# Seven half-token products in place of eight for nine of the 22 gate-and-up tiles of a feed-forward block

## The chip, the cores and the metric

The kernel runs on one NeuronCore of a Trainium2 chip. The metric is the device time of one execution in microseconds (us); lower is better. TensorE (PE) multiplies; its weight loads (PEld) are shown apart from its matmuls. VectorE (DVE), ScalarE (ACT) and GpSimd (POOL) do the elementwise work, and SyncE (SP) issues most transfers.

## The reference

The reference is two blocks, each of two layers, on 512 tokens of width 1024 in float32. The first block has a recurrent layer and a top-k attention layer. The second has a windowed attention and a sparse attention, each followed by a feed-forward layer. Only the two feed-forward layers are touched here:

```python
def rms_norm(x, g):
    x32 = x.astype(jnp.float32)
    y = x32 * lax.rsqrt(jnp.mean(x32 * x32, axis=-1, keepdims=True) + RMS_EPS)
    return (y * g.astype(jnp.float32)).astype(x.dtype)

def swiglu(h, w_gu, w_down):
    gate, up = jnp.split(h @ w_gu, 2, axis=-1)
    return (jax.nn.silu(gate) * up) @ w_down

# per layer of the second block:  h = h + mixer(...);  h = h + swiglu(rms_norm(h, ffn_norm), w_gu, w_down)
```

The hidden width is 2816, which is 22 tiles of 128. So each layer has 22 gate tiles, 22 up tiles, and a down product of 22 k-tiles onto eight output tiles.

## The kernel before

All activations lie transposed: a tile is 128 features (partitions) by 512 tokens. `X[k]`, k = 0 to 7, is the residual. `Norm` holds `n.xh[k]` and `n.xl[k]`: the residual times the norm's gain, split into a rounded high part and a low remainder, each a 128x512 tile in the fast matmul type. `n.RB` is the reciprocal root-mean-square of each token, spread over the partitions; it is multiplied in after the product.

A weight tile of 1024 rows by 128 columns comes from HBM as one 128x1024 `raw` tile (512 KB, one transfer on SP's queue). It is cut into two pieces of four k-tiles (512 columns). Of each piece ACT writes the rounded high part `wh` (L133) and DVE or GpSimd the remainder `wl = raw - wh` (L134; `wpool["l"]` lists the engines, in the feed-forward layers DVE alone). The pairs (`wh`, `wl`) rotate through numbered slots: four common ones that live for the whole kernel and a number for each layer (`hl` in `open_layer`, here 4, so 8 slots); `raw` has 2 + 2 buffers.

`dense` multiplies one weight tile by eight k-tiles. For every k-tile `mm3` (L152 to L154) issues three matmuls into one PSUM bank: high by high, high by low, low by high. So a tile costs 24 matmuls with 512 moving columns.

`ffn` (L1402) is called twice. `hidden(j)`, j = 0 to 21, makes a gate product `pg` and an up product `pu` (48 matmuls). Then DVE makes g = pg*RB (L1411), ACT tanh(g/2) (L1413), DVE th = (th+1)*g (L1414), u = pu*RB (L1416) and u = th/2*u (L1417), and `split` makes the pair `hh` (ACT, L113) and `hl` (DVE, L114). `down(k0, k1, last)` multiplies a range of hidden tiles by the down weights (`dn`) and adds to `X[m]`. The order is hidden 0 to 9, down over hidden 0 to 7, hidden 10 to 17, down over 8 to 15, hidden 18 to 21, down over 16 to 21. The second layer's last down is `down_out`, in which four output tiles are made in halves of 256 tokens and the final norm follows.

Six PSUM banks (`mm`) serve the products, two (`at`) the small ones. `tmp` gives 128x512 tiles out of eight; `hh` and `hl` have 13 buffers each. The order of instructions on each engine is made by a planner that simulates the engines and picks, among what it takes to be ready, the earliest in program order; slots come free by release. So the planner, not the chip, fixes each engine's queue.

Of the kernel before, what the change touches and what calls it, by code (L numbers as in the profile page):

```python
# [10 lines left out]
F32 = mybir.dt.float32  # L11
F32R = mybir.dt.float32r
BF16 = mybir.dt.bfloat16
AF = mybir.ActivationFunctionType
ALU = mybir.AluOpType
AX = mybir.AxisListType.X
P = 128
T = 512
NB = 4
KD = 8  # L20
# [6 lines left out]
def f32(ap):  # L27
    return ap.bitcast(F32)
# [3 lines left out]
def kernel(ctx: ExitStack, tc: tile.TileContext, a: dict, out: bass.AP, upto: int = 9, start: int = 1):  # L32
    nc = tc.nc
    pe, act, dve, pool = nc.tensor, nc.scalar, nc.vector, nc.gpsimd
# [5 lines left out]
    wpool = {"ext": None, "raw": 0, "hl": 0, "nr": 0, "np": 0}  # L40
    fetched = []
    copies = []
    st = ctx.enter_context(tc.tile_pool(name="st", bufs=2))
# [9 lines left out]
    X = [XA[:, k] for k in range(KD)]  # L53
# [4 lines left out]
    def V(name, i=0, n=1, rows=slice(None)):  # L58
        o = VEC[name][0] + i
        return vec[rows, o:o + n]  # L60
# [39 lines left out]
    def ps_mm(name):  # L100

        return bank(min(psum["mm"], key=used.index), name)
# [9 lines left out]
    def split(h, l, src, eng=None):  # L112
        act.copy(h, src)  # L113
        (eng or dve).tensor_sub(l, src, f32(h))  # L114

    PC = 512

    def wtile(kind, n, dt, tags):

        base, extra = {"raw": (2, wpool["raw"]), "hl": (4, wpool["hl"])}[kind]  # L120
        c = wpool["n" + kind] = wpool.get("n" + kind, -1) + 1
        common = c % (base + extra) < base
        return [(wg if common else wpool["ext"]).tile([P, n], dt, tag=t, name=t, bufs=base if common else extra)
                for t in tags]
# [31 lines left out]
    def dense(src, xh, xl, name="mm", M=P, w=None, mid=None, among=()):  # L156

        kt = len(xh)
        h, l = w or wload(src, kt * P)
        ps = ps_mm(name)  # L160

        def part(k0, k1):
            for k in range(k0, k1):
                mm3(ps[:M], h(k * P, M), l(k * P, M), xh[k], xl[k], k == 0, k == kt - 1)

        if among:
            with tc.manual_schedule(engines={pe.engine}):
                for k in range(kt):
                    part(k, k + 1)
                    for fn in among[k * len(among) // kt:(k + 1) * len(among) // kt]:  # L170
                        fn()
            return ps
        part(0, kt // 2)
        with tc.issue_after(mid().ins) if mid else ExitStack():
            part(kt // 2, kt)
        return ps
# [62 lines left out]
    def open_layer(name, raw, hl, tmps, roles, tw=T, weng=None):  # L239
        wpool["l"] = weng or [dve]  # L240
        es = ExitStack()
        set_banks(**roles)
        if raw or hl:
            wpool["ext"] = es.enter_context(tc.tile_pool(name=name + "w", bufs=1))
        wpool["raw"], wpool["hl"], wpool["nraw"], wpool["nhl"] = raw, hl, -1, -1
        lp = es.enter_context(tc.tile_pool(name=name, bufs=1))
        tp = es.enter_context(tc.tile_pool(name=name + "t", bufs=tmps))

        def tmp(nm, w=T):
            return tp.tile([P, tw], F32, tag="t", name=nm)[:, :w]  # L250

        return es, lp, tmp
# [1147 lines left out]


    def ffn(n, layer, gname, goff, after):  # L1402
        es, lp, tmp = open_layer(f"f{layer}", 2, 4, 8, dict(mm=6, at=2))
        H = []
        nx = Norm()

        def hidden(j):
            pg = dense(a[f"w_gu{layer}"][2 * j], n.xh, n.xl, "pg")
            pu = dense(a[f"w_gu{layer}"][2 * j + 1], n.xh, n.xl, "pu")
            g = tmp("g")  # L1410
            dve.tensor_mul(g, pg, n.RB)  # L1411
            th = tmp("th")
            act.activation(th, g, AF.Tanh, scale=0.5)  # L1413
            dve.scalar_tensor_tensor(th, th, 1.0, g, op0=ALU.add, op1=ALU.mult)  # L1414
            u = tmp("u")
            dve.tensor_mul(u, pu, n.RB)  # L1416
            dve.scalar_tensor_tensor(u, th, 0.5, u, op0=ALU.mult, op1=ALU.mult)  # L1417
            h = lp.tile([P, T], F32R, tag="hh", name="hh", bufs=13)
            l = lp.tile([P, T], F32R, tag="hl", name="hl", bufs=13)
            split(h, l, u)  # L1420
            H.append((h, l))

        def down(k0, k1, last):
            def step(m, w):
                hs = H[k0:k1]
                ps = dense(None, [x[0] for x in hs], [x[1] for x in hs], "dn", w=w)
                add_res(m, ps)
                if last:
                    norm_add(nx, m, gname, goff)

            steps = [(lambda m=m: wload(a[f"w_dn{layer}"][m][:, k0 * P:k1 * P], (k1 - k0) * P),
                      lambda w, m=m: step(m, w)) for m in range(KD)]
            if last:
                run_steps(steps, after)
            else:
                for _ in range(KD):
                    run_step(steps)

        def down_out(k0, k1):


            w = {}
            rb = st.tile([P, T], F32, tag="RB", name="RB", bufs=1)

            def load(m):
                w[m] = wload(a[f"w_dn{layer}"][m][:, k0 * P:k1 * P], (k1 - k0) * P)

            def product(m, c, wd):
                hs = H[k0:k1]
                ps = ps_mm("dn")[:, :wd]  # L1450
                for i, (xh, xl) in enumerate(hs):
                    mm3(ps, w[m][0](i * P, P), w[m][1](i * P, P), xh[:, c:c + wd], xl[:, c:c + wd], i == 0,
                        i == len(hs) - 1)
                x = X[m][:, c:c + wd]
                dve.tensor_add(x, ps, x)
                sq = st.tile([P, T], F32, tag="acc" if m == 0 else "sq", name="sq", bufs=2)
                act.activation(sq[:, c:c + wd], x, AF.Square)
                if m == 0 or m == KD - 1:
                    nx.sq.append(sq)
                else:  # L1460
                    pool.tensor_add(nx.sq[0][:, c:c + wd], nx.sq[0][:, c:c + wd], sq[:, c:c + wd])
                act.activation(x, x, AF.Identity, scale=V(gname, m))

            def rms(c, wd):
                pb, _ = bcast_cols(lambda b: nx.stat[:, b:b + 1].to_broadcast([P, P]), "nrb", wd // P, ps_mm)
                act.copy(rb[:, c:c + wd], pb[:, :wd])
                return pb

            def out_half(c, wd, pb, on_pool):
                for k in range(KD):  # L1470
                    x = X[k][:, c:c + wd]
                    if k in on_pool:
                        pool.tensor_mul(x, x, rb[:, c:c + wd])
                    else:
                        dve.tensor_mul(x, x, pb[:, :wd])
                    if k % 2:
                        q = nc.sync if k % 4 == 1 else nc.scalar
                        q.dma_start(out[:, k - 1:k + 1, c:c + wd], XA[:, k - 1:k + 1, c:c + wd])

            load(0)  # L1480
            for m in range(KD):
                if m < KD - 1:
                    load(m + 1)
                if m < 4:
                    product(m, 0, T)
            with tc.manual_schedule(engines={pe.engine}):
                for m in range(4, KD):
                    product(m, 0, T // 2)
                for m in range(4, KD):
                    if m == 5:  # L1490
                        norm_stat(nx, 0, NB // 2)
                    if m == 6:
                        half = rms(0, T // 2)
                    if m == KD - 1:
                        nx.sq.pop()
                    product(m, T // 2, T // 2)
                norm_stat(nx, NB // 2, NB // 2)
                out_half(0, T // 2, half, (1,5))
                out_half(T // 2, T // 2, rms(T // 2, T // 2), (1,5))

        for j in range(10):
            hidden(j)
        down(0, 8, False)
        for j in range(10, 18):
            hidden(j)
        down(8, 16, False)
        for j in range(18, 22):
            hidden(j)
        if after:
            down(16, 22, True)  # L1510
        else:
            down_out(16, 22)
        es.close()
        return nx
# [359 lines left out]
    if start <= 1:  # L1874
        n = even()
    else:
        es, lp, tmp = open_layer("b", 0, 0, 4, dict(mm=1, at=2))
# [4 lines left out]
        n = Norm()  # L1882
# [17 lines left out]
    if start <= 5:  # L1900
        n = nsa(n)
# [150 lines left out]
```

## Time and profile before

| | |
|---|---|
| time, median of 3 runs (lowest, highest) | 1929.52 us (1928.89, 1931.39) |
| time of the profiled execution | 1933.06 us |
| its span from first to last instruction | 1931.3 us |
| mean granted TensorE clock | 0.994 of full speed |
| busy: PE, DVE, ACT, POOL | 98%, 65%, 50%, 29% of the span |
| chain that ended last: PE, DVE | 83%, 10% of the span |

The profile shows one execution. The time holds 1.8 us beside the span. A busy share is the time in which an engine has an instruction in flight; matmuls overlap in a pipeline, so what one costs is read from the starts of neighbours, not from its length.

### The profile page before, as it was taken

How to read it: one execution, taken by the hardware profiler on the slowest of the kernel's cores; microseconds unless marked ns; L12 is line 12 of the kernel's file. 1: busy time of each engine (PE TensorE's matmuls, PEld its weight loads, DVE VectorE, ACT ScalarE, POOL GpSimd, SP SyncE). 2: the span in 40 equal slices, each digit the busy share in tenths (PEclk: the TensorE clock that was granted, in tenths of full speed). 3: DMA queues.
4: the chain of work that ended last, by engine and by line, in shares of the span. 5: the costliest groups of instructions: out<-in, count | busy, mean ns of one | idle time of the engine just before them, and what ended most of it. 6: DMA issues, size and time to landing. Idle time of an engine off the chain costs nothing.

```text
span 1931.3 us, 27214 instructions
## 1 busy us (share of the span) xinstructions
PE 1889.9 (98%) x9686; PEld 1588.1 (82%) x9686; DVE 1260.8 (65%) x2586; ACT 959.4 (50%) x1975; POOL 566.9 (29%) x622
## 2 busy tenths in 40 slices
PE   9999999999998999999999999998999999999998
PEld 7888888887788887878888888888888888888887
DVE  6776667556797778796554453557999665445443
ACT  6543344424447786785332332347888543223223
POOL 1101001124457575886000000056666420000002
PEclk9999999999999999999999999999999999999999
DMA  4233342222345553211333233243111142233221
GB/s 164 87 104 119 121 123 88 89 87 78 90 131 141 146 173 116 90 44 58 139 99 98 89 97 98 66 134 116 55 60 33 44 142 90 96 98 98 94 76 60
DMA packets 72687, 189.91 MB, mean 98 GB/s; under 512 B 9252, under 2 KB 24100, under 8 KB 72552
## 3 DMA queue, kind: packets, MB, share of 16 engines
q1 hardware_dynamic: 68824, 184.43, 30.3%
q10 hardware_dynamic: 3728, 3.75, 0.6%
q8 instruction: 76, 1.25, 0.3%
q14 instruction: 59, 0.48, 0.1%
HBM read 167.03 MB, written 12.59 MB: 93 GB/s over the span
## 4 chain that ended last, share of the span: by engine, by line
PE 83%; DVE 10%; ACT 2%; DMA 2%; issue 1%; POOL 1%; SPq 1%; DVEq 0%; ACTq 0%; POOLq 0%
PE pj L152 6%; PE pj L153 6%; PE pj L154 6%; PE pg L153 4%; PE pg L152 4%; PE pg L154 4%; PE pu L152 4%; PE pu L154 4%; PE pu L153 4%; PE dn L153 4%; PE dn L152 4%; PE dn L154 4%; PE wo L152 4%; PE wo L153 3%; PE wo L154 3%; PE po L779 2%
## 5 line engine op out<-in xcount | busy, mean ns | idle before, releaser
L133 ACT CAST wh<-raw 128x512 fp32r<-128x512 f32 (+1 forms) x582 | 353.1, 611 | 616.4 <-PE dn L153 140.5
L134 DVE TENSOR_TENSOR wl<-raw,wh 128x512 fp32r<-128x512 f32 (+2 forms) x436 | 301.3, 695 | 198.6 <-ACT wh L133 191.6
L152 PE MATMUL pj<-xh,wh 128*128 128x512 f32 (+1 forms) x648 | 265.3, 410 | 0.5 <-ACT wh L133 0.5
L154 PE MATMUL pj<-xh,wl 128*128 128x512 f32 (+1 forms) x648 | 255.2, 394 | 1.4 <-DVE wl L134 0.9
L153 PE MATMUL pj<-xl,wh 128*128 128x512 f32 (+1 forms) x648 | 255.2, 394 | 1.0 <-DVE xl L281 1.0
L134 POOL TENSOR_TENSOR wl<-raw,wh 128x512 fp32r<-128x512 f32 x146 | 197.6, 1357 | 129.8 <-ACT wh L133 109.3
L289 POOL TENSOR_TENSOR sq<-sq 128x512 f32<-128x512 f32 x27 | 43.2, 1602 | 369.9 <-ACT sq L287 369.6
L154 PEld LDWEIGHTS pj<-xh,wl 128*128 128x128 f32 (+1 forms) x648 | 121.5, 188 | 29.7 <-DVE wl L134 1.3
L153 PEld LDWEIGHTS pj<-xl,wh 128*128 128x128 f32 (+1 forms) x648 | 122.2, 189 | 24.0 <-DVE xl L281 2.4
L153 PE MATMUL dn<-hl,wh 128*128 128x512 f32 (+1 forms) x376 | 141.6, 377 | 0.0
L152 PE MATMUL dn<-hh,wh 128*128 128x512 f32 (+1 forms) x376 | 141.2, 377 | 0.0
L154 PE MATMUL dn<-hh,wl 128*128 128x512 f32 (+1 forms) x376 | 140.7, 375 | 0.0
L152 PEld LDWEIGHTS pj<-xh,wh 128*128 128x128 f32 (+1 forms) x648 | 122.1, 188 | 22.3 <-ACT wh L133 1.6
L152 PE MATMUL pg<-xh,wh 128*128 128x512 f32 x352 | 138.2, 393 | 0.0
L153 PE MATMUL pg<-xl,wh 128*128 128x512 f32 x352 | 138.2, 393 | 0.0
L154 PE MATMUL pg<-xh,wl 128*128 128x512 f32 x352 | 138.2, 393 | 0.0
L152 PE MATMUL pu<-xh,wh 128*128 128x512 f32 x352 | 138.0, 392 | 0.0
L154 PE MATMUL pu<-xh,wl 128*128 128x512 f32 x352 | 138.0, 392 | 0.0
L153 PE MATMUL pu<-xl,wh 128*128 128x512 f32 x352 | 137.9, 392 | 0.0
L152 PE MATMUL wo<-yh,wh 128*128 128x512 f32 x320 | 130.7, 409 | 2.3 <-DVE vv L114 1.4
L153 PE MATMUL wo<-yl,wh 128*128 128x512 f32 x320 | 125.9, 395 | 0.0
L154 PE MATMUL wo<-yh,wl 128*128 128x512 f32 x320 | 125.7, 395 | 0.0
(413 smaller groups left out, 4401.1 us busy)
## 6 DMA issues: line engine op xcount, KB each, us to landing
raw<-in_w_gu SPq DMA_DIRECT2D x88, 512.0 KB, 3.5
raw<-in_w_even SPq DMA_DIRECT2D x48, 512.0 KB, 3.6
raw<-in_w_dn SPq DMA_DIRECT2D x32, 512.0 KB, 3.6
rsc<-rv SPq DMA_DIRECT2D x64, 160.0 KB, 3.7
raw<-in_w_eout SPq DMA_DIRECT2D x16, 512.0 KB, 3.6
stp<-rsc SPq DMA_DIRECT2D x32, 256.0 KB, 3.2
raw<-in_w_odd SPq DMA_DIRECT2D x13, 512.0 KB, 3.7
raw<-in_w_dn SPq DMA_DIRECT2D x16, 384.0 KB, 3.1
```

The costliest lines, as they stand in the source:

```text
L133: act.copy(h[:, :m], raw[:, o:o + m])
L134: eng[i % len(eng)].tensor_sub(l[:, :m], raw[:, o:o + m], f32(h[:, :m]))
L152: pe.matmul(ps, wh, xh, start=first, stop=False)
L153: pe.matmul(ps, wh, xl, start=False, stop=False)
L154: pe.matmul(ps, wl, xh, start=False, stop=last)
L289: (eng or (dve if k == KD - 1 else pool)).tensor_add(n.sq[0], n.sq[0], sq)
L779: pe.matmul(dst[:, :, 256 - w:], vv(b), p[:, :, 256 * b:256 * b + w], start=start and x + b == 0, stop=stop and x == 1 and b == nb - 1)
```

## The change

Nine of the 22 hidden tiles, j = 5, 7, 9, ..., 21, take another way to gate and up. The product is seen as a 2x2 by 2x2 block product: the two rows of blocks are gate and up, the inner index is the even or odd k-tile of a pair, and the two columns are the first and second 256 tokens. Seven block products (Strassen's scheme in its form with few additions) replace eight. Each block product is four k-tile pairs of three matmuls with 256 moving columns, so a tile has 84 such matmuls for 48 with 512.

- `scheme_weights` loads the same two raw tiles, forms four sums of weight blocks (s1 and a new a21 on GpSimd, s2 and a new a12 on DVE) and splits seven 512-column parts: seven casts on ACT, four remainders on DVE and three on GpSimd.
- `token_sums(q)`, called once for each k-tile pair in hidden 0 to 3, forms the four token-side sums: two scalings on ACT, four 128x256 subtractions on GpSimd, two splits of 512 columns.
- After the seven products ACT copies one half and DVE does seven 128x256 additions or subtractions that each read PSUM, into g and u. GpSimd multiplies g by RB and DVE u by RB; the rest of `hidden` stays.
- From j = 6 on the weight remainders of the other tiles and of the down products alternate between DVE and GpSimd.
- Eight slots for weight pairs become ten, 8 `tmp` tiles become 6, 13 `hh`/`hl` buffers become 11. The token sums take 4 x 2 tiles of 128x1024. In the other 13 tiles u = pu*RB now stands ahead of the tanh in program order.

```diff
     def ffn(n, layer, gname, goff, after):
-        es, lp, tmp = open_layer(f"f{layer}", 2, 4, 8, dict(mm=6, at=2))
+        es, lp, tmp = open_layer(f"f{layer}", 2, 6, 6, dict(mm=6, at=2))
...
+        def token_sums(q):
+            xe, xo, ta, tb = (tmp(nm) for nm in ("xe", "xo", "ta", "tb"))
+            for x, k in ((xe, 2 * q), (xo, 2 * q + 1)):
+                act.activation(x, X[k], AF.Identity, scale=V("ffn_norm", KD * layer + k))
+            t1, t2, t3, t4 = ta[:, :HT], ta[:, HT:], tb[:, :HT], tb[:, HT:]
+            pool.tensor_sub(t1, xe[:, HT:], xe[:, :HT])
+            pool.tensor_sub(t3, xo[:, HT:], xe[:, HT:])
+            pool.tensor_sub(t2, xo[:, HT:], t1)
+            pool.tensor_sub(t4, t2, xo[:, :HT])
+            h = lp.tile([P, 2 * T], F32R, name=f"th{q}")
+            l = lp.tile([P, 2 * T], F32R, name=f"tl{q}")
+            split(h[:, :T], l[:, :T], ta)
+            split(h[:, T:], l[:, T:], tb)
...
+        def scheme_weights(j):
...
+            def part(src, eng):
+                h, l = wtile("hl", PC, F32R, ("wh", "wl"))
+                hv, lv = (t.rearrange("p (q c) -> p q c", c=P) for t in (h, l))
+                act.copy(hv, src)
+                eng.tensor_sub(lv, src, f32(hv))
+                w.append((h, l))
+
+            pool.tensor_add(s1, a21, a22)
+            part(a11, dve)
+            part(a12, pool)
+            dve.tensor_sub(s2, s1, a11)
+            part(s1, dve)
+            pool.tensor_sub(a21, a11, a21)
+            part(s2, dve)
+            part(a21, pool)
+            dve.tensor_sub(a12, a12, s2)
+            part(a22, pool)
+            part(a12, dve)
...
+            for pair in plan:
+                ps = ps_mm("pw")
+                for y, rhs in enumerate(pair):
+                    h, l = w.pop(0)
+                    d = ps[:, y * HT:y * HT + HT]
+                    for q in range(KD // 2):
+                        c = slice(q * P, q * P + P)
+                        xh, xl = rhs(q)
+                        pe.matmul(d, h[:, c], xh, start=y == q == 0, stop=False)
+                        pe.matmul(d, h[:, c], xl, start=False, stop=False)
+                        pe.matmul(d, l[:, c], xh, start=False, stop=y == len(pair) - 1 and q == KD // 2 - 1)
+                    P7.append(d)
+            p1, p2, p5, p6, p7, p4, p3 = P7
...
+            act.copy(u0, p1)
+            dve.tensor_add(g0, p2, u0)
+            dve.tensor_add(u1, p6, u0)
+            dve.tensor_add(g1, p5, u1)
+            dve.tensor_add(u0, p7, u1)
+            dve.tensor_add(u1, p7, g1)
+            dve.tensor_sub(u0, u0, p4)
+            dve.tensor_add(g1, p3, g1)
 
         def hidden(j):
...
+            if j >= 5 and j % 2:
+                g, u = scheme(j)
+                pool.tensor_mul(g, g, n.RB)
+                dve.tensor_mul(u, u, n.RB)
+            else:
+                if j == 6:
+                    wpool["l"] = [dve, pool]
...
+            if j < 4:
+                token_sums(j)
...
-            h = lp.tile([P, T], F32R, tag="hh", name="hh", bufs=13)
-            l = lp.tile([P, T], F32R, tag="hl", name="hl", bufs=13)
+            h = lp.tile([P, T], F32R, tag="hh", name="hh", bufs=11)
+            l = lp.tile([P, T], F32R, tag="hl", name="hl", bufs=11)
```

## Rows read from the trace of the kernel before

**Rows 1.** Page, busy time: engine, us, share of span, instructions
```profile
PE 1889.9 (98%) x9686; PEld 1588.1 (82%) x9686; DVE 1260.8 (65%) x2586; ACT 959.4 (50%) x1975; POOL 566.9 (29%) x622
```

**Rows 2.** Page, chain that ended last, by engine
```profile
PE 83%; DVE 10%; ACT 2%; DMA 2%; issue 1%; POOL 1%; SPq 1%; DVEq 0%; ACTq 0%; POOLq 0%
```

**Rows 3.** Windows: an attention stretch, hidden 10 to 17, a down product
```profile
core 0: us, PE busy (x) PEld busy (x) DVE busy (x) ACT busy (x) POOL busy (x), PEclk, DMA share, GB/s
...
640.00:680.00 40.00, 39.30 (x280) 35.31 (x280) 27.78 (x75) 28.96 (x69) 22.18 (x20) 1.00 0.47 125
...
1069.00:1157.00 88.00, 88.00 (x383) 71.72 (x383) 46.11 (x70) 29.10 (x47) 0.00 (x0) 1.00 0.30 96
...
1157.00:1201.00 44.00, 44.00 (x194) 36.23 (x193) 17.11 (x26) 10.57 (x18) 0.00 (x0) 1.00 0.31 96
```

**Rows 4.** Timeline of PE: first matmuls of hidden 10, 11 and 12
```profile
1068.82 0.39 PE L152 MATMUL pg<-xh,wh 128*128 128x512 f32 x1
...
1080.02 0.40 PE L152 MATMUL pg<-xh,wh 128*128 128x512 f32 x1
...
1090.93 0.40 PE L152 MATMUL pg<-xh,wh 128*128 128x512 f32 x1
```

**Rows 5.** Timeline of PE: 90 half-width matmuls, 1902.65 to 1913.20
```profile
1902.65 0.28 PE L152 MATMUL dn<-hh,wh 128*128 128x256 f32 x1
...
1903.00 0.28 PE L152 MATMUL dn<-hh,wh 128*128 128x256 f32 x1
...
1903.24 0.28 PE L154 MATMUL dn<-hh,wl 128*128 128x256 f32 x1
...
1907.30 0.28 PE L152 MATMUL dn<-hh,wh 128*128 128x256 f32 x1
...
1907.64 0.28 PE L152 MATMUL dn<-hh,wh 128*128 128x256 f32 x1
...
1913.20 0.95 PE L310 MATMUL nst<-cst,sq 128*128 128x2 f32 x8
```

**Rows 6.** Timeline of weight loads in the same stretch
```profile
1903.12 0.19 PEld L154 LDWEIGHTS dn<-hh,wl 128*128 128x128 f32 x1
```

**Rows 7.** Groups of DVE, hidden 10 to 17: count, busy us, mean ns, idle before
```profile
L134 DVE TENSOR_TENSOR wl<-raw,wh 128x512 fp32r<-128x512 f32 x32 | 22.0, 687 | 11.1 <-ACT wh L133 11.1
...
L1416 DVE TENSOR_TENSOR u<-pu,RB 128x512 f32<-128x512 f32 x7 | 4.8, 691 | 11.2 <-PE pu L154 11.2
```

**Rows 8.** Groups of ACT, hidden 10 to 17
```profile
L133 ACT CAST wh<-raw 128x512 fp32r<-128x512 f32 x32 | 19.9, 622 | 46.6 <-PE pu L153 24.8 <-PE pg L153 19.3 <-PE dn L153 2.1
```

**Rows 9.** Groups of DVE and POOL by shape, 1880 to 1931
```profile
L1455 DVE TENSOR_TENSOR x<-dn,x 128x256 f32<-128x256 f32 x8 | 3.4, 424 | 11.4 <-PE dn L154 11.4
...
L1461 POOL TENSOR_TENSOR sq<-sq 128x256 f32<-128x256 f32 x6 | 4.4, 739 | 7.5 <-ACT sq L1457 7.5
L1461 POOL TENSOR_TENSOR sq<-sq 128x512 f32<-128x512 f32 x3 | 3.9, 1307 | 334.4 <-ACT sq L1457 334.4
```

**Rows 10.** Timeline of DVE around 465, while POOL works
```profile
458.87 1.79 DVE L134 TENSOR_TENSOR wl<-raw,wh 128x512 fp32r<-128x512 f32 x1
460.58 1.78 DVE L281 SCALAR_TENSOR_TENSOR xl<-x,vec,xh 128x512 fp32r<-128x512 f32 x1
...
468.65 0.68 DVE L323 TENSOR_TENSOR x<-wo,x 128x512 f32<-128x512 f32 x1
```

**Rows 11.** Timeline of POOL in the same stretch
```profile
465.18 1.74 POOL L289 TENSOR_TENSOR sq<-sq 128x512 f32<-128x512 f32 x1
466.89 1.29 POOL L134 TENSOR_TENSOR wl<-raw,wh 128x512 fp32r<-128x512 f32 x1
```

**Rows 12.** Timeline of DVE and PE after the last up product
```profile
1886.39 0.69 DVE L1416 TENSOR_TENSOR u<-pu,RB 128x512 f32<-128x512 f32 x1 [1.55 <-PE pu L154]
...
1888.70 0.69 DVE L114 TENSOR_TENSOR hl<-u,hh 128x512 fp32r<-128x512 f32 x1 [0.69 <-ACT hh L113]
...
1889.63 0.39 PE L152 MATMUL dn<-hh,wh 128*128 128x512 f32 x1
```

More of the change, by code (lines that the diff above doesn't have):

```diff
@@ L1402, in ffn @@
     def ffn(n, layer, gname, goff, after):
-        es, lp, tmp = open_layer(f"f{layer}", 2, 4, 8, dict(mm=6, at=2))
+        es, lp, tmp = open_layer(f"f{layer}", 2, 6, 6, dict(mm=6, at=2))
         H = []
         nx = Norm()
-        def hidden(j):
[L1408 to L1411, printed above, removed]
+        HT = T // 2
+        sums = []
@@ new lines, in token_sums @@
+        def token_sums(q):
[11 more added lines that the diff above has]
+            split(h[:, T:], l[:, T:], tb)
+            sums.append((h, l))
@@ new lines, in scheme_weights @@
+        def scheme_weights(j):
+            raws = []
+            for m in (2 * j, 2 * j + 1):
+                raw, = wtile("raw", 1024, F32, ("raw",))
+                nc.sync.dma_start(raw, a[f"w_gu{layer}"][m])
+                raws.append(raw.rearrange("p (q e c) -> p e q c", e=2, c=P))
+            (a11, a12), (a21, a22) = ((r[:, 0], r[:, 1]) for r in raws)
+            s1 = st.tile([P, T], F32, tag="acc", name="s1", bufs=2).rearrange("p (q c) -> p q c", c=P)
+            s2 = st.tile([P, T], F32, tag="sq", name="s2", bufs=2).rearrange("p (q c) -> p q c", c=P)
+            w = []
+            def part(src, eng):
[15 more added lines that the diff above has]
+            part(a12, dve)
+            return w
@@ new lines, in scheme, with xs, ts @@
+        def scheme(j):
+            w = scheme_weights(j)
+            def xs(k, c):
+                return n.xh[k][:, c:c + HT], n.xl[k][:, c:c + HT]
+            def ts(q, i):
+                return tuple(t[:, i * HT:i * HT + HT] for t in sums[q])
+            plan = ((lambda q: xs(2 * q, 0), lambda q: xs(2 * q + 1, 0)), (lambda q: ts(q, 0), lambda q: ts(q, 1)),
+                    (lambda q: ts(q, 2), lambda q: ts(q, 3)), (lambda q: xs(2 * q + 1, HT),))
+            P7 = []
+            for pair in plan:
[11 more added lines that the diff above has]
+            p1, p2, p5, p6, p7, p4, p3 = P7
+            g, u = tmp("g"), tmp("u")
+            g0, g1, u0, u1 = g[:, :HT], g[:, HT:], u[:, :HT], u[:, HT:]
+            act.copy(u0, p1)
[6 more added lines that the diff above has]
+            dve.tensor_add(g1, p3, g1)
+            return g, u
@@ new lines, in hidden @@
+        def hidden(j):
+            if j >= 5 and j % 2:
[5 more added lines that the diff above has]
+                    wpool["l"] = [dve, pool]
+                pg = dense(a[f"w_gu{layer}"][2 * j], n.xh, n.xl, "pg")
+                pu = dense(a[f"w_gu{layer}"][2 * j + 1], n.xh, n.xl, "pu")
+                g, u = tmp("g"), tmp("u")
+                dve.tensor_mul(g, pg, n.RB)
+                dve.tensor_mul(u, pu, n.RB)
+            if j < 4:
+                token_sums(j)
@@ L1414, in hidden @@
             dve.scalar_tensor_tensor(th, th, 1.0, g, op0=ALU.add, op1=ALU.mult)
-            u = tmp("u")
-            dve.tensor_mul(u, pu, n.RB)
             dve.scalar_tensor_tensor(u, th, 0.5, u, op0=ALU.mult, op1=ALU.mult)
-            h = lp.tile([P, T], F32R, tag="hh", name="hh", bufs=13)
-            l = lp.tile([P, T], F32R, tag="hl", name="hl", bufs=13)
+            h = lp.tile([P, T], F32R, tag="hh", name="hh", bufs=11)
+            l = lp.tile([P, T], F32R, tag="hl", name="hl", bufs=11)
             split(h, l, u)
```

## The prediction

> **What bounds the kernel now.** I read the page's busy shares and its chain first, then the windows of the feed-forward stages, then the timeline of PE in them. PE is busy for 98% of the span and is 83% of the chain that ended last [rows 1, 2]. The reader is to see in the windows that the feed-forward stages are the extreme case: PE is busy for 88.0 of 88 us at a granted clock of 1.00 (the 2.4 GHz level), while DVE has work for 46.1 us, ACT for 29.1 and POOL for none [rows 3]. ACT's weight casts there wait mostly for a PE matmul that frees a slot, 46.6 us for 32 of them [rows 8]: the weights are made ahead, and PE waits for nobody. So in these stages time is the number of matmuls times their distance, and the other engines' spare time is what the change can spend.
>
> **What the change removes on PE.** The distance comes from the starts. Hidden 10 takes 1080.02 - 1068.82 = 11.20 us, hidden 11 takes 1090.93 - 1080.02 = 10.91 [rows 4]; over 48 matmuls that is 233.3 and 227.3 ns. The alternation runs through all the later tiles, 233 ns in even ones and 227 in odd ones, so each of the nine tiles that change costs 10.91 now.
>
> For 256 moving columns the second layer's last down product has the same kind of matmul, same types and full weights: 90 of them between 1902.65 and 1913.20, 10.55 / 90 = 117.2 ns. Within it two levels are seen, (1903.24 - 1903.00) / 2 = 120 and (1907.64 - 1907.30) / 3 = 113.3 [rows 5]. A changed tile then costs 84 x 117.2 ns = 9.85 us (9.52 to 10.08). It saves 10.91 - 9.85 = 1.06 us (0.83 to 1.39), not the eighth of 1.36 us that the count of multiplications promises, because the half-width matmul costs more than half a full one. Eighteen such tiles in two layers: **-19.1 us** (-14.9 to -25.0). The saving is gone at 10.91 / 84 = 129.9 ns.
>
> A weight load lasts 0.19 us [rows 6], longer than the 0.12 us between half-width matmuls, so loads overlap each other as well as the matmuls. The rows show that they keep up. The Trainium skill's page "TensorE: Matmul & The Clock Gate", section "Back-to-back issue gap", gives a sustained spacing of pairs of load and matmul of about 81 ns at 128 columns and 131 ns at 512; by a straight line between them (an estimate) 256 columns cost 98 ns, and the changed tile would take 84 x 98 = 8.2 us where the old one took 48 x 131 = 6.3. By that rule fixed costs weigh so much that halving the columns loses; the trace has 233 and 117 ns for the same two widths, so the rule isn't borne out here.
>
> **The 26 tiles that stay.** Their two distances go with something that alternates from tile to tile, and the weight slots do so: eight slots, four for each tile. With ten slots and seven taken by a changed tile the places shift. No row tells which places give the shorter distance. If all come to 227 ns, some 22 tiles gain 0.29 us each, -6.4; if all come to 233, four tiles lose as much, +1.2. I take **-1.0**, a mixture with a few more at 227.
>
> **What the change adds, against PE's time.** A pair of one changed and one normal tile gives PE 9.85 + 11.20 = 21.05 us. In it:
> - ACT has 7 + 4 casts, 2 tanh, 2 `hh` casts at about 0.62 [rows 8] and a half-width copy, below 10 us. Half of its time stays free.
> - DVE has in the changed tile four remainders, two weight sums, u*RB, two steps of silu and `hl`: ten operations with both inputs in SBUF; in the normal tile two remainders, two steps and `hl`: five. At 0.69 [rows 7] that is 10.4 us. The seven half-width operations that read PSUM take 0.42 each [rows 9], 3.0, and g and u of the normal tile 1.4. Sum 14.7 us.
> - POOL has two sums, three remainders and g*RB, then two remainders: eight of about 1.31 [rows 9], 10.5 us.
>
> By these numbers alone every engine fits: DVE 70%, POOL 50% of PE's time. But DVE and POOL disturb each other. Where POOL works beside DVE, a DVE remainder takes 1.79 us and a scaled one 1.78, while an addition with one input in PSUM keeps 0.68 [rows 10]; POOL's own operations there take 1.74, and 1.29 when left alone [rows 11]. An operation of DVE with two SBUF inputs and one of POOL thus follow each other. The Trainium skill's page "SBUF — State Buffer", section "Who interferes with whom", states this as a lock: such a DVE instruction contends with a GpSimd instruction that reads SBUF, and the second one waits for the whole of the first. The trace agrees, with 1.79 for 0.69.
>
> The price: if each of the eight POOL operations held up one DVE operation by 1.79 - 0.69 = 1.1 us, DVE would need 14.7 + 8.8 = 23.5 us, 2.4 more than PE's 21.05; if half do, 19.1, and PE still sets the pace. Bounds over 18 pairs: 0 to +43 us. Two things pull it to the low end. DVE is free of two-input work for a third of the pair, and ten slots let weights run some six parts ahead, so only a lasting overload reaches PE. The nearest stretch with both engines loaded has DVE at 27.8 and POOL at 22.2 of 40 us, nearly these shares, and PE still at 39.3 [rows 3]. I take **+2**. Each down product, in which DVE is busy 17.1 of 44 us [rows 3], lets both engines catch up.
>
> **Token sums.** Four calls in a layer, each four ACT passes (2.5 us or a little over), four POOL operations of 0.74 [rows 9] (3.0) and two DVE remainders (1.4), in hidden 0 to 3, where PE takes over 10.9 us a tile. The spare ACT and DVE time covers them, and hidden 5 is the first user. Where the layer begins, the norm uses the same engines; if that cover is gone, the first call delays RB or the first weights by some 1 us. I take **+1** for both layers (0 to +3).
>
> **The end of hidden 21.** It changes, and the down product needs it. Now the end of the up product (PE turns to `dn` before 1886.39) is followed by u*RB at 1886.39 and `hl` at 1888.70 to 1889.39, while PE uses tiles 16 to 20 and comes to a sixth at 1889.63 [rows 12]: it arrives with 0.2 us to spare. The new chain behind the last product is an addition (0.42), g*RB on POOL (1.31), tanh, two steps, cast and remainder (0.63 + 0.69 + 0.69 + 0.62 + 0.69), 5.1 us and some 0.6 between engines, against 3.0 now. Up to 2.4 us would be late next, PE's sixth k-tile, if the queue keeps its order. The planner has five other output tiles to put in front, each 15 matmuls of 0.23 us that need only tiles 16 to 20, so the cover can be long. Between 0 and +4.8 for two layers; I take **+1**.
>
> Nothing else is on the path: the bytes and the number of transfers stay, SP's queue gets no new work, but a raw tile of a changed j is held until its last part is made. With four raw buffers the next two transfers start then, one tile (about 10 us) before they are needed. The buffers cut from 8 to 6 and 13 to 11 hold at most ten live hidden tiles and one more; only ACT or POOL would wait.
>
> **Sum.** -19.1 - 1.0 + 2 + 1 + 1 = -16.1 us. On the profiled execution's own 1933.06 that is 1917.0. It stood 3.5 above the median of the runs, so against the median: 1929.5 - 16.1 = **1913 us**, 0.8% faster. This case by itself spans 1904 to 1921: -25.0 with nothing lost, to half of the saving given back.
>
> **Rivals.**
> 1. *DVE and POOL become the bound (slower).* Place: the pairs from j = 5 on. Price: up to 2.4 us a pair, more if ACT casts also wait behind POOL's sums s1 and a21. It decides from 1.0 us for each changed tile, where 18 us are eaten. At the bound: 1929.5 - 19.1 + 1.0 + 43 = 1954. For it: DVE two-input work (10.4) and POOL work (10.5) add up to 20.9 of 21.05 us if they strictly take turns. Against: in alternation a pair of them took about 1.75, not 0.69 + 1.31, and PE held 39.3 of 40 under a like load. Full bound 0.10. A middle form, in which some 0.4 to 1.0 us a tile is lost, gives 1921 to 1931: 0.14.
> 2. *The half-width matmul costs more here than in the down product*, because weight loads surface when two token operands and seven parts alternate. If nothing overlapped, 84 x 0.19 = 16.0 us a tile, +5.0 each, 2021 in all; at 126 ns, 10.6 us a tile, the saving shrinks to 6, and the result is near 1927. Against: loads of 0.19 at a distance of 0.12 [rows 5, 6]. Chance 0.05, mostly in "same".
> 3. *More is gained*: places turn to the shorter distance, for changed and normal tiles alike: -25.0 - 6.4, about 1899. No row speaks for it beyond the existence of that distance. Chance 0.06.
>
> The forecast has 0.65. A difference of 0.2% (3.9 us) is about what a measurement of this kernel tells from none: 1925.7 to 1933.4 counts as same. Faster: forecast 0.65, more gained 0.06, half of the middle form and a little of rival 2, together 0.80. Same: 0.09. Slower: 0.11. The range that leaves out the top of rival 1 and the lowest of rival 3: 1903 to 1929.
>
> **What would show it.** In the profile of the changed kernel: 84 matmuls of 256 columns in the rows of `pw`, at 113 to 120 ns, 9.5 to 10.1 us from the first of one tile to the next tile's; if 130, the first step is wrong. POOL busy some 10 us in each pair, DVE remainders and silu steps up to 1.8 us. If PE's row has idle time ahead of `pw` or `pg` with `wl` as releaser, the DVE and POOL step is wrong; idle time ahead of `dn` with `hl` as releaser is the end of hidden 21. The forecast fails if the idle time in one changed tile is above 1 us.

## The result and the profile after

The changed kernel takes 1910.74 us (median of 4 runs, 1909.29 to 1911.10) beside 1930.45 us for the kernel before on the same chip: ratio 0.9896, 95% interval 0.9884 to 0.9908, that is 1.04% or some 20 us faster. The forecast was 1913 in a range of 1903 to 1929. The profiled execution took 1910.72 us, its span 1909.0. In the experiments below one of four executions with all 17 tiles took 2448 us and two of six with thirteen tiles 1926 and 2036, at a lower granted clock (0.69, 0.93 and 0.85); the medians count them, and the ratio for thirteen tiles holds the 1926.

The page's busy shares answer to [rows 1]; the line under them is the chain, for [rows 2].

```profile
PE 1868.6 (98%) x10334; PEld 1603.1 (84%) x10334; DVE 1360.1 (71%) x2666; ACT 1005.0 (53%) x2079; POOL 863.8 (45%) x842
...
PE 85%; DVE 8%; ACT 2%; DMA 1%; POOL 1%; issue 1%; SPq 0%; DVEq 0%; POOLq 0%; ACTq 0%
```

PE has 648 more matmuls (18 tiles with 84 for 48) and is busy for 21 us less; POOL has 297 us more. The windows show the four pairs of hidden 10 to 17, one by one, then the stretch as a whole, then a down product. The columns are length, the busy time of PE, PEld, DVE, ACT and POOL with the number of instructions, the granted clock, and the share and rate of DMA.

```profile
1062.64:1083.60 20.96, 20.96 (x133) 19.00 (x132) 13.05 (x19) 8.07 (x14) 9.12 (x7) 1.00 0.30 101
1083.60:1104.63 21.03, 21.03 (x134) 18.99 (x133) 15.84 (x23) 9.00 (x16) 11.62 (x9) 1.00 0.31 101
1104.63:1125.71 21.08, 21.08 (x134) 18.96 (x133) 15.89 (x23) 8.66 (x16) 10.92 (x8) 1.00 0.31 101
1125.71:1146.50 20.79, 20.79 (x134) 18.61 (x133) 18.11 (x28) 9.12 (x17) 10.81 (x8) 1.00 0.37 105
1062.64:1146.50 83.86, 83.86 (x529) 75.55 (x528) 62.90 (x90) 34.85 (x62) 42.47 (x29) 1.00 0.33 102
...
1018.95:1062.64 43.69, 43.69 (x194) 36.05 (x193) 19.65 (x26) 11.20 (x18) 16.27 (x12) 1.00 0.31 97
```

A pair takes 20.8 to 21.1 us, all of it PE. DVE went from 52% of this stage [rows 3] to 75%, POOL from nothing to 51%. The timeline of PE shows two changed tiles from their first matmul to the next product's: 1083.60 - 1073.62 = 9.98 us and 1146.50 - 1136.92 = 9.58, or 118.8 and 114.0 ns for each of 84.

```profile
1073.62 0.28 PE L1482 MATMUL pw<-xh,wh 128*128 128x256 f32 x1
...
1083.60 0.40 PE L152 MATMUL pg<-xh,wh 128*128 128x512 f32 x1
...
1136.92 0.28 PE L1482 MATMUL pw<-xh,wh 128*128 128x256 f32 x1
...
1146.50 0.39 PE L152 MATMUL dn<-hh,wh 128*128 128x512 f32 x1
```

The groups of DVE and POOL by shape in hidden 10 to 17 answer to [rows 7, 9, 10, 11]: `wl` is a weight remainder, `th` a step of silu, `g<-pw,u` an addition that reads PSUM.

```profile
L134 DVE TENSOR_TENSOR wl<-raw,wh 128x512 fp32r<-128x512 f32 x11 | 10.9, 990 | 0.0
L1516 DVE SCALAR_TENSOR_TENSOR th<-th,g 128x512 f32<-128x512 f32 x7 | 10.5, 1493 | 5.5 <-ACT th L1515 5.5
...
L1490 DVE TENSOR_TENSOR g<-pw,u 128x256 f32<-128x256 f32 x4 | 1.7, 418 | 0.0
...
L134 POOL TENSOR_TENSOR wl<-raw,wh 128x512 fp32r<-128x512 f32 x10 | 15.0, 1508 | 7.4 <-ACT wh L133 7.4
...
L1502 POOL TENSOR_TENSOR g<-g,RB 128x512 f32<-128x512 f32 x3 | 5.0, 1669 | 5.0 <-DVE g L1496 5.0
```

The silu step in the kernel before, in the same stretch:

```profile
L1414 DVE SCALAR_TENSOR_TENSOR th<-th,g 128x512 f32<-128x512 f32 x8 | 5.5, 693 | 0.8
```

In the two groups of DVE with two SBUF inputs shown the mean went from 0.69 to 0.99 and 1.49 us (others, such as `hl`, stay at 0.69); the half-width ones with an input in PSUM stay at 0.42. The two engines hold each other up as forecast; but the view of PE's waits is empty over both feed-forward layers.

**Where the time went, stage by stage.** From the starts on PE's timeline (first `pg` of a layer, first `pj` behind it, last `dn`), in us, for profiled executions:

| kernel | to layer 1 | layer 1 | between | layer 2 to last `dn` | rest |
|---|---|---|---|---|---|
| before | 907.4 | 370.7 | 275.8 | 366.9 | 10.5 |
| after | 904.6 | 360.5 | 276.5 | 356.7 | 10.7 |
| frame alone | 905.6 | 371.0 | 281.9 | 367.2 | 11.0 |
| eight half-width products | 904.7 | 373.2 | 278.0 | 369.4 | 10.5 |
| no sums formed | 902.5 | 360.5 | 276.4 | 356.7 | 10.6 |
| all 17 tiles | 903.6 | 383.9 | 276.9 | 382.6 | 10.5 |
| remainders on GpSimd | 904.5 | 360.5 | 275.9 | 356.7 | 10.5 |
| no GpSimd | 902.6 | 360.5 | 276.5 | 356.8 | 10.5 |
| eleven tiles | 905.9 | 358.6 | 283.0 | 354.7 | 10.5 |
| thirteen tiles | 904.9 | 356.1 | 276.5 | 355.4 | 11.1 |
| thirteen, no GpSimd | 903.9 | 355.8 | 276.6 | 352.0 | 10.5 |
| thirteen, mixed | 904.7 | 355.8 | 276.4 | 352.0 | 11.1 |

The layers gain 10.2 us each, 20.4 in all. They repeat to 0.1 us where the instructions on PE are the same; the attention stages, which the change doesn't touch, move by several us from one kernel or execution to the next. So what a variant does is read from the two layer columns.

### The profile page after: what moved, and what is told of

Read it like the earlier page. It is cut to its first block, busy times and chain, and to the rows that moved or that the text cites. A ratio compares the mean times of both kernels' runs of the same rounds, so it can differ in the third digit from the quotient of the medians.

```text
span 1909.0 us, 29335 instructions
## 1 busy us (share of the span) xinstructions
PE 1868.6 (98%) x10334; PEld 1603.1 (84%) x10334; DVE 1360.1 (71%) x2666; ACT 1005.0 (53%) x2079; POOL 863.8 (45%) x842
## 4 chain that ended last, share of the span: by engine, by line
PE 85%; DVE 8%; ACT 2%; DMA 1%; POOL 1%; issue 1%; SPq 0%; DVEq 0%; POOLq 0%; ACTq 0%
PE pj L152 7%; PE pj L153 6%; PE pj L154 6%; PE dn L153 4%; PE dn L152 4%; PE dn L154 4%; PE wo L152 4%; PE wo L154 4%; PE wo L153 4%; PE pw L1484 3%; PE pw L1483 3%; PE pw L1482 3%; PE pu L154 3%; PE pu L153 3%; PE pu L152 3%; PE pg L152 3%
## 5 line engine op out<-in xcount | busy, mean ns | idle before, releaser
L133 ACT CAST wh<-raw 128x512 fp32r<-128x512 f32 (+1 forms) x510 | 306.5, 609 | 396.4 <-PE pj L153 120.8
L134 POOL TENSOR_TENSOR wl<-raw,wh 128x512 fp32r<-128x512 f32 (+1 forms) x226 | 303.5, 1346 | 247.6 <-ACT wh L133 225.1
L134 DVE TENSOR_TENSOR wl<-raw,wh 128x512 fp32r<-128x512 f32 (+1 forms) x284 | 222.1, 788 | 109.8 <-ACT wh L133 103.9
L1444 POOL TENSOR_TENSOR wl<-raw,wh 128x512 fp32r<-128x512 f32 x54 | 76.1, 1410 | 103.5 <-ACT wh L1443 92.4
L744 ACT ACTIVATE L<-L,sm 128x128 f32<-128x128 f32 (+1 forms) x192 | 107.4, 561 | 18.9 <-DVE sm L742 17.8
L742 DVE CUSTOM_DVE_ANT_0 L<-lg,stp 128x128 f32<-128x128 f32 (+1 forms) x192 | 87.6, 482 | 6.3 <-PE lg L796 2.8
L114 DVE TENSOR_TENSOR pl<-pt,ph 128x384 fp32r<-128x384 f32 (+1 forms) x144 | 83.3, 592 | 10.6 <-ACT ph L113 9.3
L1443 ACT CAST wh<-raw 128x512 fp32r<-128x512 f32 x90 | 55.3, 618 | 64.7 <-PE dn L153 33.7
L580 POOL TENSOR_TENSOR up<-u 128x527 f32<-128x527 f32 x8 | 11.1, 1387 | 170.1 <-DVE nq L535 79.5
L323 DVE TENSOR_TENSOR x<-wo,x 128x512 f32<-128x512 f32 x88 | 60.2, 686 | 34.3 <-PE wo L154 33.8
```

The costliest lines, as they stand in the source:

```text
L133: act.copy(h[:, :m], raw[:, o:o + m])
L134: eng[i % len(eng)].tensor_sub(l[:, :m], raw[:, o:o + m], f32(h[:, :m]))
L323: dve.tensor_add(X[k], ps, X[k])
L742: dve.tensor_tensor_reduce(L, lg, strip[:, (1 - ii) * P:], 1.0, -NEG, op0=ALU.add, op1=ALU.min, accum_out=sm[:, ii:ii + 1])
L744: act.activation(L, L, AF.Exp, scale=-1.0, bias=sm[:, ii:ii + 1], accum_out=sm[:, 2 + ii:3 + ii])
L1444: eng.tensor_sub(lv, src, f32(hv))
```

## The experiments

Ratios are to the kernel before on the same chip. The theory is the prediction's: PE's matmuls times their distance set the time, everything else is hidden as long as DVE, held up by GpSimd, keeps pace. The rivals: part of the gain is the frame's; or the sums cost PE time; or the engines don't hold each other up enough to matter.

**The frame alone.** Slots, buffers and the sharing of remainders as in the change, but no changed tile and no token sums.

```diff
-            if j >= 5 and j % 2:
+            if False:
...
-            if j < 4:
+            if False:
                 token_sums(j)
```

> The change's frame without its scheme: ten weight slots, 6 temporaries, 11 hidden buffers, and weight remainders shared by DVE and GpSimd from hidden 6 on, but all 22 hidden tiles by eight full-width products and no token sums. My theory: PE still never waits, so only the distances between matmuls can change; in the changed kernel the 26 unchanged tiles gave back about 1 us a layer, so 1928 to 1930 for 1930.5 before, 0 to -2.5. Rival (part of the gain is the frame's: shared remainders or more slots let PE run closer): 1921 or below, and the scheme is worth less than 10 us.

Measured: 1932.71 us, ratio 1.0017 (1.0006 to 1.0027). That lies above the expected 1928 to 1930. The frame gains nothing: each layer is 0.3 us longer than before. The other 2 us of the median aren't in the feed-forward layers; in the profiled execution the excess is in the attention stage between them, and its cause stays open. The distances have a period of ten slots now. On PE's timeline, from the first matmul of each product to that of the next:

```profile
1111.64 0.40 PE L152 MATMUL pg<-xh,wh 128*128 128x512 f32 x1
...
1117.24 0.39 PE L152 MATMUL pu<-xh,wh 128*128 128x512 f32 x1
...
1122.71 0.39 PE L152 MATMUL pg<-xh,wh 128*128 128x512 f32 x1
...
1128.14 0.40 PE L152 MATMUL pu<-xh,wh 128*128 128x512 f32 x1
```

The products take 5.60, 5.47 and 5.43 us: 233, 228 and 226 ns. Over the layer three products at 233 and two at 227 follow each other. Counted in program order, the two are those whose weights lie in the four common slots. That fits the alternation before (four and four), except that hidden 1, whose weights have common slots in both kernels, runs at 233.

**Eight products at half width** in the nine tiles, on the same frame.

```diff
-                g, u = scheme(j)
-                pool.tensor_mul(g, g, n.RB)
-                dve.tensor_mul(u, u, n.RB)
+                pg, pu = halves(2 * j, "ph"), halves(2 * j + 1, "ph")
+                g, u = tmp("g"), tmp("u")
+                dve.tensor_mul(g, pg, n.RB)
+                dve.tensor_mul(u, pu, n.RB)
# halves: wload as ever; for each of two 256-token halves, 8 k-tiles x 3 matmuls into its half of one bank
```

> The frame of the first run, and in the nine tiles eight products of 256 tokens in place of the seven: the same two weight tiles, each multiplied by the first and then by the second 256 tokens, 96 half-width matmuls for 48, no sums of any kind. My theory (a half-width matmul costs 113 to 120 ns, 117.2 on the mean): 96 x 117.2 = 11.25 us a tile against 10.9 to 11.2, so 0 to +0.35 a tile, 0 to +7 in all: 1930 to 1936. With the changed kernel's 118 ns the seven products then save 12 x 118 = 1.4 us a tile against this run, 25 us in all. Rival (half width costs more wherever weights change with each matmul, and the scheme's gain came from elsewhere): above 1940.

Measured: 1938.64 us, ratio 1.0043 (1.0028 to 1.0058), above the expected 1930 to 1936, of which the frame's own 1932.7 is a part. A tile:

```profile
1078.01 0.28 PE L1508 MATMUL ph<-xh,wh 128*128 128x256 f32 x1
...
1089.32 0.40 PE L152 MATMUL pg<-xh,wh 128*128 128x512 f32 x1
```

11.31 us, 117.8 ns for each of 96. Against the frame the layers are 2.2 us longer each: that is the price of halving the width, 0.24 us a tile. Against this run the seven products are 12.7 us shorter in each layer, 1.41 a tile, which is the twelve matmuls left out at 118 ns (1.42). The changed tiles alone are 204.5 - 177.8 = 26.7 us shorter over both layers, 1.48 each; the other products give 0.6 us a layer back. So within 0.1 us a tile the gain is the eighth product, less the price of the width.

**No sums formed.** The four token subtractions and the four weight sums are left out; the parts are made of plain blocks.

```diff
-            pool.tensor_add(s1, a21, a22)
...
-            dve.tensor_sub(s2, s1, a11)
-            part(s1, dve)
-            pool.tensor_sub(a21, a11, a21)
-            part(s2, dve)
+            part(a21, dve)
+            part(a22, dve)
...
-            dve.tensor_sub(a12, a12, s2)
# and the four pool.tensor_sub of token_sums
```

> The changed kernel without the forming of sums: the four token subtractions on GpSimd and the four weight sums (two on GpSimd, two on DVE) are left out, and the parts are made of plain blocks, so gate and up are not the reference's; all casts, remainders, matmuls and additions behind the products stay. My theory (all of this work is hidden under PE): the same as the changed kernel, 1909 to 1912. Rival (the sums, by DVE and GpSimd taking turns, cost PE some of its time): down to 1900 or so, 0.4 to 0.6 us for each of 18 tiles.

Measured: 1910.45 us, ratio 0.9898 (0.9881 to 0.9914). Both layers take what they take with the sums, 360.5 and 356.7 us, though DVE and POOL have much less to do in nearly the same stretch:

```profile
1062.00:1146.00 84.00, 84.00 (x530) 75.68 (x529) 49.50 (x85) 35.55 (x62) 33.90 (x24) 1.00 0.36 110
```

DVE 49.5 us for 62.9, POOL 33.9 for 42.5, and not 0.1 us on PE. The forming of the sums is hidden wholly.

**All 17 tiles from hidden 5 on.**

```diff
-            if j >= 5 and j % 2:
+            if j >= 5:
...
-                if j == 6:                 # where the sharing of remainders begins
+                if j == 4:
```

> All 17 tiles from hidden 5 on take the scheme, no normal tile between them to give the other engines air. My theory (DVE and GpSimd follow each other where both read SBUF twice): a changed tile has DVE 10 x 0.69 + 7 x 0.42 = 9.8 us of its own and six GpSimd operations of 1.31, six of which hold up a DVE operation by up to 1.1: 9.8 to 16 us, likely 12 to 14, for 9.9 of PE. PE waits 2 to 4 us a tile behind the weight remainders, less what the down products let them get ahead: 8 more tiles a layer at -1.2, 17 tiles at about +2: 1910 - 19 + 68 = about 1960, from 1920 to 2000, with idle PE ahead of the seven products. Rival (the engines don't hold each other up enough to matter): PE keeps 9.9 us a tile and the time is 1910 - 16 x 1.2 = 1891.

Measured: 1960.57 us, ratio 1.0152 (1.0135 to 1.0169), slower than before. The time is the one expected, the cause mostly another. Here the cover is gone. The view of PE's waits over the first layer gives what PE waited for, the sum, the count and the longest:

```profile
PE pw L1482 <- DVE g L1490: 11.8, 6, 2.3
PE pw L1484 <- DVE wl L1444: 3.7, 3, 1.3
PE dn L152 <- ACT hh L113: 2.6, 1, 2.6
```

The first line isn't the weights, which I had expected. `g<-pw,u` (L1490) is the first DVE operation behind a tile's products, and it releases a PSUM bank; PE waits for a bank because DVE is behind. The windows of the changed tiles of the three stages:

```profile
966.14:1025.29 59.15, 53.32 (x421) 52.36 (x420) 57.23 (x73) 23.86 (x46) 35.65 (x23) 0.94 0.25 75
1069.09:1166.51 97.42, 85.45 (x673) 83.56 (x672) 90.98 (x115) 36.80 (x70) 65.51 (x40) 0.95 0.25 77
1210.25:1249.84 39.59, 39.59 (x338) 39.58 (x336) 34.68 (x48) 15.75 (x30) 24.84 (x17) 1.00 0.23 69
```

Five tiles take 59.15 us (11.8 each), eight 97.42 (12.2), DVE at 97 and 93%. The granted clock of these two stretches is 0.94 and 0.95: after its waits PE ran part of the time at 1.2 GHz, so the lost time is waits and clock together. Of the 27.9 us above 13 tiles of 9.9, PE was idle for 17.8. The last four take 9.9 each without a wait; they stand behind a down product, in which the engines can get ahead, and the queue then waits at the end, for `hh`. DVE in the second stretch, on its timeline:

```profile
1087.81 1.78 DVE L1516 SCALAR_TENSOR_TENSOR th<-th,g 128x512 f32<-128x512 f32 x1
1089.52 1.78 DVE L1450 TENSOR_TENSOR s<-s,raw 128x512 f32<-128x512 f32 x1
1091.22 0.41 DVE L1490 TENSOR_TENSOR g<-pw,u 128x256 f32<-128x256 f32 x1
```

A step of silu and a weight sum at 1.78 us stand in DVE's queue ahead of the short addition on which a bank depends.

**Every remainder on GpSimd.**

```diff
-            part(a11, dve)          # likewise s1, s2 and the last a12
+            part(a11, pool)
...
-                    wpool["l"] = [dve, pool]
+                    wpool["l"] = [pool]
```

> The changed kernel with every weight remainder on GpSimd from hidden 5 on: 14 GpSimd operations in a pair of tiles for 8, nine DVE operations with two SBUF inputs for 15. The engines' own sums fall on DVE (15 less 6 operations of 0.69) and come to 14 x 1.31 = 18.3 us on GpSimd, for 20.9 of PE. My theory (the two take turns): nine DVE operations each push GpSimd back by about 0.44, 18.3 + 4.0 = 22.3 us, 1.4 above PE's time in each of 18 pairs, less what the down products let them get ahead: 1915 to 1935, with PE waiting for remainders made by GpSimd. Rival (each engine has its own way and only its own sum counts): 1911, no waits.

Measured: 1910.84 us, ratio 0.9901 (0.9888 to 0.9914), no waits. My expectation fell. In hidden 10 to 17:

```profile
1062.50:1146.00 83.50, 83.50 (x527) 75.16 (x526) 53.58 (x60) 32.00 (x59) 70.84 (x48) 1.00 0.31 95
```

POOL is busy for 70.8 us with 48 operations, 1.48 each: they do stretch, but by 0.2 us over 1.29, not 0.28, and eight of the 56 that I had counted for four pairs lie outside the stretch. 85% is short of the bound. The run doesn't refute that the engines take turns (the next one shows that they do); it shows that the price was less than I took it for.

**No GpSimd in the scheme's weights.** All sums, remainders and g*RB on DVE.

```diff
-            pool.tensor_add(s1, a21, a22)      # likewise every pool in scheme_weights
+            dve.tensor_add(s1, a21, a22)
...
-                    wpool["l"] = [dve, pool]
+                    wpool["l"] = [dve]
...
-                pool.tensor_mul(g, g, n.RB)
+                dve.tensor_mul(g, g, n.RB)
```

> The changed kernel with all its weight sums, remainders and g*RB on DVE; GpSimd keeps only the token sums. DVE has 23 operations of 0.69 with two SBUF inputs, seven of 0.42 and two of 0.69 in a pair, 20.2 us by their lengths, about 17.6 by the distance of their starts when they follow closely (0.61), for 20.9 of PE; no GpSimd operation to wait for. My theory (an operation of DVE is long only because it waits for GpSimd): remainders come down from 0.99 to 1.03 to 0.69 us, DVE just fits, 1910 to 1914, so that GpSimd's help is worth little here. Rival (DVE's eight more operations make it the bound): 1918 to 1935.

Measured: 1908.63 us, ratio 0.9894 (0.9881 to 0.9907), the layers unchanged. In the same stretch, the windows and two groups of DVE:

```profile
1062.50:1146.00 83.50, 83.50 (x528) 75.22 (x528) 68.04 (x119) 35.67 (x62) 0.00 (x0) 1.00 0.37 113
```
```profile
L134 DVE TENSOR_TENSOR wl<-raw,wh 128x512 fp32r<-128x512 f32 x21 | 14.4, 686 | 2.2 <-ACT wh L133 1.7
...
L1516 DVE SCALAR_TENSOR_TENSOR th<-th,g 128x512 f32<-128x512 f32 x7 | 4.8, 684 | 0.0
```

With GpSimd silent the remainders are back at 0.69 us and the silu step at 0.68, from 0.99 and 1.49: the length was GpSimd's doing. And DVE, with 29 more operations, is busy only 68.0 us for 62.9. At the edges of such a stretch different operations fall in, so the price is read over the whole first layer; the windows are those of the changed kernel, of the run with every remainder on GpSimd, and of this one:

```profile
904.56:1265.06 360.50, 360.50 (x1949) 311.61 (x1948) 235.90 (x321) 146.51 (x255) 169.54 (x126) 1.00 0.32 97
...
904.50:1265.00 360.50, 360.50 (x1949) 311.60 (x1948) 210.61 (x245) 143.23 (x255) 276.21 (x202) 1.00 0.32 98
...
902.60:1263.10 360.50, 360.50 (x1949) 311.56 (x1948) 253.73 (x415) 148.38 (x255) 37.19 (x32) 1.00 0.32 97
```

POOL has 94 operations more than here in the first and 170 in the second, DVE as many fewer. So each operation given to GpSimd relieved DVE by (253.73 - 235.90) / 94 = 0.19 us, and by (253.73 - 210.61) / 170 = 0.25 where more are given, and most of them take 0.61 to 0.69 on DVE itself.

**Eleven tiles**, with hidden 10 and 18, **and thirteen**, two changed and one normal.

```diff
-            if j >= 5 and j % 2:
+            if j in (5, 7, 9, 10, 11, 13, 15, 17, 18, 19, 21):                # eleven
+            if j in (5, 6, 8, 9, 10, 11, 13, 14, 16, 17, 18, 19, 21):         # thirteen
...
-                if j == 6:
+                if j == 4:                                                    # thirteen
```

> Eleven changed tiles in a layer: hidden 10 and 18 take the scheme too, the first tiles behind a down product, whose weights can be made while the down product runs. My theory (cover is what decides): the run with all 17 tiles showed four changed tiles in a row at 9.9 us each right behind a down product, so both are free: 4 x (9.9 - 11.1) = -4.8 us, 1904 to 1908. Rival (two changed tiles in a row are already too much for DVE, which takes some 12.2 us for each): 1910 or above.

> Thirteen changed tiles in a layer: two changed, one normal, with the last two of each stage changed where a down product follows that doesn't need them; the last three are changed, normal, changed. My theory: DVE's time for a changed tile under full load is 12.2 us (from the run with all 17 tiles), for a normal one 5 to 6; two and one give 30 us, PE takes 9.9 x 2 + 11.1 = 30.9, so DVE just keeps up: 8 x -1.2 = -9.6, 1899 to 1905. Rival (without a normal tile after each changed one the order of DVE's work makes PE wait): 1905 to 1915.

Measured: eleven 1908.00 us, ratio 0.9891 (0.9877 to 0.9905); thirteen 1904.83, 0.9890 (0.985 to 0.993). The layers give 1.9 and 2.0 us for eleven (2.4 each expected), 4.4 and 1.3 for thirteen (4.8 each). The second layer of thirteen lost 3.4 us where hidden 8 and 9 follow each other: 1648.67 - 1625.31 = 23.36 us for the two, where such pairs take 19.6 to 20.2 elsewhere. PE's waits in that layer, all in or right behind these two tiles:

```profile
PE pw L1484 <- DVE wl L1444: 1.3, 2, 1.1
PE dn L152 <- DVE u L1495: 0.6, 1, 0.6
PE pw L1484 <- POOL wl L1444: 0.3, 1, 0.3
```

These are 1.6 us for remainders and 0.6 for a bank, 2.2 of the 3.4; the rest isn't accounted for. Two changed tiles in a row is where the margin gets thin with this use of GpSimd; why the first layer's pair got through (20.24 us, no wait in the view) stays open.

**Thirteen tiles with less of GpSimd.** First all on DVE, then a mixture in which GpSimd keeps the remainders of a12 and a22 and half of the normal tiles' ones.

```diff
# thirteen tiles, and as in the run without GpSimd; the mixture leaves these:
             part(a12, pool)
...
             part(a22, pool)
...
                     wpool["l"] = [dve, pool]
```

> Thirteen changed tiles as before, but all weight sums, remainders and g*RB of them on DVE as in the run without GpSimd. From that run DVE needs 68.0 / 4 = 17.0 us for a changed and a normal tile, of which the normal one is 9 x 0.61 = 5.5: 11.5 for a changed one. Two and one: 28.5 us for 30.9 of PE. My theory (GpSimd's operations, by holding DVE up, cost nearly what they take off it): no waits of PE, 8 x -1.2 against the changed kernel, 1899 to 1903. Rival (without GpSimd's help DVE falls behind where two changed tiles follow each other): 1905 to 1915 with PE waiting for remainders.

> Thirteen changed tiles; GpSimd takes only the remainders of a12 and a22 and half of the normal tiles' and the down products' remainders; the weight sums, a21's remainder and g*RB, for which ACT or DVE wait, go to DVE. My theory: fewer waits behind GpSimd's sums and 0.2 to 0.3 us of DVE saved by each of the operations left there, so a little more air than with DVE alone: no waits of PE, 1899 to 1903, within 2 us of the run on DVE alone. Rival (each GpSimd operation holds up DVE by more than it saves): PE waits as in the first run with thirteen tiles, 1903 to 1908.

Measured: 1901.33 us, ratio 0.9849 (0.9836 to 0.9862), and 1901.61, 0.9848 (0.9835 to 0.9862). Both beat the changed kernel (0.9896) by some 0.5%, with intervals that don't meet. The first one's windows of the changed stages:

```profile
967.00:1018.00 51.00, 51.00 (x385) 48.97 (x384) 48.59 (x92) 26.30 (x47) 0.00 (x0) 1.00 0.37 116
1062.00:1143.00 81.00, 81.00 (x596) 76.76 (x595) 74.28 (x138) 39.52 (x69) 0.00 (x0) 1.00 0.38 112
```

DVE is at 95 and 92% and PE waits for nothing. Both layers gain all that the count of tiles promises, 4.7 us for four tiles at 1.2.

## Why the prediction was right

The forecast of -16.1 us stands beside -19.7 between the medians. Over the two layers, by the prediction's steps:

| term | forecast | measured |
|---|---|---|
| 18 changed tiles | -19.1 | -18.6 |
| 26 other tiles and the down products | -1.0 | -1.8 |
| DVE and GpSimd | +2 | 0 |
| token sums | +1 | 0 |
| end of hidden 21 | +1 | 0 |
| all | -16.1 | -20.4 |

The miss is mostly in the last three terms: they were allowances for waits, +4 in all, and no wait came.

*The changed tiles.* The distance read from the second layer's last down product, 117.2 ns, came out at 114.0 to 118.8 in the tiles shown; the 18 tiles add up to 177.8 us for 196.4, 117.6 ns on the mean. The run with eight half-width products shows that this is the number of products and next to nothing else. Rival 2, a dearer half-width matmul, is out. The Trainium skill's page "TensorE: Matmul & The Clock Gate" (section "Back-to-back issue gap") has the two sustained spacings between which the prediction drew its line (an estimate), by which the tile would have lost; 117.6 ns for 227 to 233 doesn't bear it out.

*The other tiles.* The sign and cause were right, the size was not: even tiles, at 233 ns before from hidden 2 on, meet places with 227 now in some of their products. That at 512 columns the place of the weight slots goes with the distance is shown by the frame's new period; what in the place sets it isn't, and hidden 1 doesn't fit.

*DVE and GpSimd.* The mechanism is shown, with 0.99 and 1.49 us beside GpSimd and 0.69 and 0.68 without it. The Trainium skill's page "SBUF — State Buffer" (section "Who interferes with whom") states it for DVE instructions with two SBUF inputs; the trace agrees. Its price on PE was mis-sized, +2 where 0 was measured: with a normal tile after each changed one DVE is at 75%. Rival 1 is real and lies further on: with all 17 tiles DVE reaches 93 to 97% and the kernel is slower than before by 1.5%. That run named a dependence the prediction didn't have: the wait is for a PSUM bank that a late DVE hasn't read, not mainly for weights.

*Token sums, end of hidden 21.* Both cost nothing. From the first layer's first `pg` to the start of hidden 5, behind all four calls, PE takes 62.6 us before and after, and leaving the subtractions out changes no layer by 0.1 us. The chain behind the last product is longer than counted, 6.5 us for 5.7: the addition starts at 1864.12, g*RB takes 1.74 us on POOL instead of 1.31, and `hl` is done at 1870.65, 7.0 us after PE turned to `dn` at 1863.62.

```profile
1864.12 0.42 DVE L1496 TENSOR_TENSOR g<-pw,g 128x256 f32<-128x256 f32 x1
...
1864.93 1.74 POOL L1502 TENSOR_TENSOR g<-g,RB 128x512 f32<-128x512 f32 x1
...
1869.96 0.69 DVE L114 TENSOR_TENSOR hl<-u,hh 128x512 fp32r<-128x512 f32 x1 [0.69 <-ACT hh L113]
```

PE didn't wait: the planner put other output tiles' matmuls in front. On PE's timeline the matmuls of hidden 21 are the ones that come in a bunch, here after the change and then before it:

```profile
1873.92 1.07 PE L152 MATMUL dn<-hh,wh 128*128 128x512 f32 x4
...
1893.03 0.84 PE L152 MATMUL dn<-hh,wh 128*128 128x512 f32 x3
```

After the change PE runs 45 matmuls first, five k-tiles of three output tiles, and comes to the bunch 3.3 us after `hl` is done. Before it, 30 matmuls, two output tiles, stood in front, and PE came to it 3.6 us after `hl` was done (1889.39). So the prediction misread the row at 1889.63 [rows 12]: there PE begins the next output tile, and the 0.2 us to spare were 3.6. With all 17 tiles that cover was too short (2.6 us for `hh`).

## What to carry to other kernels

Where one engine is busy without a gap, price a change by its instructions' distance for the very shape, taken from the trace; a shape of half the width costs a little more than half (118 for 233 ns here), and that took a sixth of what the product left out saves (2.2 of 12.7 us). What is added on other engines is free until one of them is nearly full, and then the loss is steep, because waits also cost clock (0.94 granted with all 17 tiles); spread such tiles evenly and put extra ones where another stage lets the engine catch up. Before giving work to a second engine, look at what it does to the first: if the two exclude each other, the help may be worth a third of the work taken over (0.19 to 0.25 of some 0.69 us here), and leaving all or most of it out made room for more.

## What the runs showed that I had not expected

At 512 columns a matmul's distance goes with where its weights lie: 226 to 228 ns for the common slots and 233 for the layer's own, hidden 1 excepted. At 256 columns there are levels as far apart, 113 and 120 ns, but the place alone doesn't set them. In the changed kernel, counted in program order, hidden 15 and hidden 17 both have four of their seven weight parts in the common slots; hidden 17 takes 9.58 us, as shown, and hidden 15 takes 1125.71 - 1115.78 = 9.93. What makes the difference stays open.

```profile
1115.78 0.28 PE L1482 MATMUL pw<-xh,wh 128*128 128x256 f32 x1
...
1125.71 0.40 PE L152 MATMUL pg<-xh,wh 128*128 128x512 f32 x1
```

Moving 94 operations of a layer, 132 us of GpSimd's time, relieved DVE by 17.8 us in all. And DVE can be 95% busy beside a PE that doesn't wait in that stretch, as with thirteen tiles and no GpSimd; with all 17 tiles, at 93 to 97%, PE waits.
